# Two directions of an mLSTM folded into one product: the weights scaled by their denominators, the denominators taken two heads at a time, projections placed between the heads

## The chip, the core and the metric

The kernel runs on one core of a Trainium2 chip. The metric is the device time of one execution in microseconds (us); lower is better. The core has an engine for matmuls (TensorE, PE in the rows, its weight loads PEld), three engines for elementwise work (VectorE, DVE; ScalarE, ACT; GpSimd, POOL) and DMA queues that SyncE (SP) issues. Each engine takes its instructions in the order in which the program lists them and waits at each for what it reads and for the buffer that it writes.

## The reference, cut to what matters

The model is a two-layer transformer-like stack over 256 context and 256 latent tokens, 1024 channels wide, batch 1. In each layer one projection feeds three branches (a bidirectional mLSTM, attention in a window, global attention), then come a merge, an output projection and a SwiGLU feed-forward block. The change lies in the mLSTM, with 4 heads of 128 channels. It is written as a scan over blocks:

```python
w = jnp.exp(dlog - m_t[..., None])
s = jnp.einsum('bhtd,bhsd->bhts', qc, kc) * w
num = a[..., None] * jnp.einsum('bhtd,bhde->bhte', qc, C) + jnp.einsum('bhts,bhse->bhte', s, vc)
den = a * jnp.einsum('bhtd,bhd->bht', qc, n) + jnp.sum(s, axis=-1)
hc = num / jnp.maximum(jnp.abs(den), jnp.exp(-m_t))[..., None]
```

It runs once forwards and once backwards in time; the two results are added and then normalised per head, gated by a tanh of another projection (B_O) and projected on. The kernel has no scan: for each head and direction it forms the whole masked matrix of weights, 512 keys by up to 512 queries. In layer 0 the queries are all 512 tokens, in layer 1 only the 256 latent ones.

## The kernel before

**The work around the change.** `layer` (from L964) runs projections with weights split into a high and a low part: `split` makes `whi` by a copy on ACT (L192) and `wlo` by a subtraction on DVE (L193), and each block of the product is three matmuls (two with `whi`, one with `wlo`), all at L135, since a helper issues every matmul. A projection of one 128-channel strip is 24 matmuls. `proj_v` makes the values `v` of all heads, in four PSUM tiles of the pools `mm`, `s`, `mm`, `s`; DVE adds a bias to each and so frees the tile (L417). In layer 0 DVE also computes the modulation vectors of the adaLN by long multiply-and-accumulate passes (L300, tiles `q`, `h`), in blocks that `mod_upto` puts into the stream between the projections; `late` counts them out.

**The mLSTM of a head.** `rep` broadcasts a row of the running maximum over the 128 partitions by a matmul into `tr`; ACT takes exponentials (L590) into eight weight tiles, four blocks of keys (`sb`) by two directions (`d`), direction 0 in `q`, direction 1 in `wk`; POOL cuts the diagonal blocks (L596, L600). PE multiplies keys and queries into `s` (shape `s<-m,m`), and DVE multiplies each score with the weight tile in place (L613). The products with the values go to two PSUM tiles, direction 0 in `acc`, direction 1 in `tr`, and ACT copies each out to `y` (L679).

**Denominators.** For heads 0 to 2 POOL first adds the four weight tiles of a direction (`mlstm_weight_sums`, L637 to L652, into `pv`), and one product with a strip of 32 columns of a constant adds the sum over keys into one of four groups of 32 partitions of a shared PSUM tile `den` (shape 128*32). Head 3 feeds its tiles directly. After the fourth head one chain makes the reciprocals `r` of all heads: copy on ACT, a matmul with C_SUM into `tr`, two DVE operations, the DVE reciprocal (L694). Then `mlstm_sum` per head: two broadcasts of `r`, two DVE multiplies and an add (L703, L704), a square on ACT (L705).

**What sets the order.** The tile framework records the program in the order in which it is written, moved by priority, and puts instructions on each engine in one fixed list. A tile pool with few buffers ties a producer to the last reader of the buffer: PSUM has 3 buffers `mm`, 2 `s`, 2 `tr`, 1 `acc`. In layer 0 the four B_O projections stand ahead of the first score; in layer 1 they come ahead of the gates. The four WQ projections and WK follow heads 2 and 3 and stand between the sums (`other`, L997).

Of the kernel before, what the change touches and what calls it, by code (L numbers as in the profile page):

```python
# [10 lines left out]
F32 = mybir.dt.float32  # L11
# [65 lines left out]
MSB = ((2, 3), (0, 1))  # L77
# [15 lines left out]
class Net:  # L93
    def __init__(self, nc, tc, es, io, out, plan=None):
# [25 lines left out]
        self.low = self.cp.tile([128, 1], F32, name="low")  # L120
        self.ident = self.cst[:, C_ID:C_ID + 128]
# [453 lines left out]

    def mlstm_weights(self, h, n, rows):
# [4 lines left out]
        wt = {}  # L581
        for d in range(2):
            mrep = self.rep(mx, d, h, n)
            for sb in ((2, 3, 0, 1) if d == 0 else (3, 2, 1, 0)):
# [4 lines left out]
                w = self.big("wk" if d else "q")  # L589
                nc.scalar.activation(out=w[:, lo:hi], in_=mrep[:, lo:hi], func=AF.Exp, scale=-1.0,  # L590
                                     bias=ut[:, 64 * sb + 32 * d + h:64 * sb + 32 * d + h + 1])
                if sb < 2 or not lat_only:
# [6 lines left out]
                    else:  # L599
                        self.masked = nc.gpsimd.affine_select(out=w[:, a:a + 128], in_=w[:, a:a + 128],  # L600
                                                              pattern=[[-1, 128]], compare_op=ALU.is_ge, fill=0.0,
                                                              base=0, channel_multiplier=1)
# [3 lines left out]
    def mlstm_scores(self, n, half, q, k, wt):  # L606
        for sb in MSB[half]:
# [8 lines left out]
    def mlstm_values(self, h, n, half, v, wt, num, den):  # L616
        parts = []
        for d in range(2):
            for i, sb in enumerate(MSB[half][::1 - 2 * d]):
                w, lo, hi = wt[d, sb]  # L620
                pieces = [(lo, hi)]
                if d == 0 and sb == 3 and n == T:
                    pieces = [(0, SEQ), (384, 512)]
                for a, b in pieces:
                    self.mm(num[d][:, a:b], v[sb][:, 128 * h:128 * h + 128], w[:, a:b], i + half == 0, i + half == 2)
                    parts.append((d, sb, w, a, b))
        if h < NH - 1:
            return
        for d, sb, w, a, b in parts:
            self.mlstm_den_part(den, h, d, sb % 2, w, a, b, half == 1)  # L630

    def mlstm_den_part(self, den, h, d, i, w, a, b, stop):

        r, c = 4 * d + h, 32 * (2 * i + d)
        self.mm(den[c:c + 32, a:b], self.cst[:, C_STRIP + 31 - r:C_STRIP + 63 - r], w[:, a:b], False, stop)

    def mlstm_weight_sums(self, n, wt):  # L637

        nc = self.nc
        t = self.t("pv", [128, 2 * T])  # L640
        sums = [t[:, :n], t[:, T:T + n]]
        for d in (1, 0):
            out = sums[d]
            order = (2, 3, 0, 1) if d == 0 else (3, 2, 1, 0)
            (w0, _, _), (w1, _, hi) = [wt[d, sb] for sb in order[:2]]
            nc.gpsimd.tensor_tensor(out=out[:, :hi], in0=w0[:, :hi], in1=w1[:, :hi], op=ALU.add)
            if hi < n:
                nc.gpsimd.tensor_copy(out[:, hi:], w0[:, hi:n])
            for sb in order[2:]:
                w, lo, hi = wt[d, sb]  # L650
                nc.gpsimd.tensor_tensor(out=out[:, lo:hi], in0=out[:, lo:hi], in1=w[:, lo:hi], op=ALU.add)
        return sums  # L652

    def mlstm_heads(self, n, q, k, v, rows, den, other):

        nums, prev = [], None
        sums = []
        for h in range(NH + 1):
            for half in range(2):
                if h < NH:  # L660
                    if half == 0:
                        wt = self.mlstm_weights(h, n, rows)
# [644 lines left out]
```

## Time and profile before

| | |
|---|---|
| runs of before | 1457.09 us median (1456.44 to 1457.2, 3 runs) |
| profiled execution | 1458.23 us, its span 1456.5 us |
| TensorE busy, share of the span | 1437.6 us, 99% |
| VectorE busy | 1065.0 us, 73% |
| ScalarE, GpSimd busy | 743.3 us and 55.4 us |
| mLSTM of layer 0 (first score to last value matmul) | about 130 to 171 us of the span |
| mLSTM of layer 1 | about 998 to 1024 us |

The profiled execution is one run with its own time; the span goes from its first to its last instruction. An engine that is busy for 99% of the span leaves hardly anything but its own work to shorten, and any time in which it is kept waiting is added to the end.

### The profile page before, as it was taken

How to read it: one execution, taken by the hardware profiler on the slowest of the kernel's cores; microseconds unless marked ns; L12 is line 12 of the kernel's file. 1: busy time of each engine (PE TensorE's matmuls, PEld its weight loads, DVE VectorE, ACT ScalarE, POOL GpSimd, SP SyncE). 2: the span in 40 equal slices, each digit the busy share in tenths (PEclk: the TensorE clock that was granted, in tenths of full speed). 3: DMA queues.
4: the chain of work that ended last, by engine and by line, in shares of the span. 5: the costliest groups of instructions: out<-in, count | busy, mean ns of one | idle time of the engine just before them, and what ended most of it. 6: DMA issues, size and time to landing. Idle time of an engine off the chain costs nothing.

```text
span 1456.5 us, 24450 instructions
## 1 busy us (share of the span) xinstructions
PE 1437.6 (99%) x8586; PEld 1224.6 (84%) x8586; DVE 1065.0 (73%) x2672; ACT 743.3 (51%) x1525; POOL 55.4 (4%) x111
## 2 busy tenths in 40 slices
PE   8999999999999999999999999999999999999997
PEld 5686687778777889888888888988889889999997
DVE  6595498667698447988688687764899867776775
ACT  4644456557853336332332233755567766655553
POOL 0003300000000000000000000004100000000000
PEclk8999999999999999999999999999999999999998
DMA  9662012222246222666455553241234335555552
GB/s 339 226 210 72 30 47 95 66 73 87 95 145 232 98 84 74 216 203 210 152 188 194 175 173 100 94 152 59 70 103 146 106 111 184 175 183 184 182 176 86
DMA packets 112587, 203.67 MB, mean 140 GB/s; under 512 B 12496, under 2 KB 16336, under 8 KB 112464
## 3 DMA queue, kind: packets, MB, share of 16 engines
q1 hardware_dynamic: 112464, 202.11, 41.7%
q8 instruction: 67, 1.10, 0.3%
q14 instruction: 56, 0.46, 0.1%
HBM read 201.02 MB, written 1.05 MB: 139 GB/s over the span
## 4 chain that ended last, share of the span: by engine, by line
PE 92%; DVE 4%; ACT 2%; issue 1%; DMA 1%; SPq 0%; ACTq 0%; DVEq 0%
PE mm L135 62%; PE s L135 20%; PE acc L135 4%; PE tr L135 4%; PE tr L788 2%; DVE wlo L193 1%; DVE q L488 1%; DMA y<-w_mod 1%; DVE y L703 0%; DVE h L447 0%; ACT q L375 0%; ACT hx L192 0%; ACT q L494 0%; DVE wk L769 0%; DMA wraw<-w_in 0%
## 5 line engine op out<-in xcount | busy, mean ns | idle before, releaser
L192 ACT ACTIVATE whi<-wraw 128x512 fp32r<-128x512 f32 (+1 forms) x558 | 345.0, 624 | 512.7 <-PE mm L135 344.2
L135 PE MATMUL mm<-hx,whi 128*128 128x512 f32 (+2 forms) x2128 | 540.9, 342 | 0.3 <-ACT wk L928 0.2
L193 DVE TENSOR_TENSOR wlo<-wraw,whi 128x512 fp32r<-128x512 f32 (+1 forms) x558 | 374.7, 680 | 163.8 <-ACT whi L192 145.7
L135 PEld LDWEIGHTS mm<-hx,whi 128*128 128x128 f32 x2128 | 365.9, 189 | 50.4 <-issue 5.2
L135 PE MATMUL mm<-hx,wlo 128*128 128x512 f32 (+2 forms) x1064 | 361.3, 340 | 0.0
L135 PE MATMUL mm<-y,whi 128*128 128x256 f32 (+1 forms) x1024 | 260.5, 332 | 0.0
L135 PEld LDWEIGHTS mm<-hx,wlo 128*128 128x128 f32 x1064 | 201.6, 190 | 23.7 <-issue 2.4
L135 PE MATMUL s<-hx,whi 128*128 128x512 f32 (+2 forms) x800 | 192.7, 330 | 0.0
L135 PEld LDWEIGHTS mm<-y,whi 128*128 128x128 f32 x1024 | 176.7, 190 | 17.0
L135 PE MATMUL mm<-y,wlo 128*128 128x256 f32 (+1 forms) x576 | 188.6, 327 | 0.0
L135 PEld LDWEIGHTS s<-hx,whi 128*128 128x128 f32 x800 | 135.9, 190 | 14.1 <-issue 0.4
L135 PE MATMUL s<-hx,wlo 128*128 128x512 f32 (+2 forms) x400 | 132.0, 330 | 0.0
L135 PEld LDWEIGHTS mm<-y,wlo 128*128 128x128 f32 x576 | 109.4, 190 | 9.5
L300 DVE SCALAR_TENSOR_TENSOR q<-q,q 128x512 f32<-128x512 f32 x160 | 105.4, 684 | 0.1
L300 DVE SCALAR_TENSOR_TENSOR h<-q,q 128x512 bf16<-128x512 f32 x160 | 104.7, 684 | 1.0 <-DMA q<-w_mod 1.0
L135 PE MATMUL mm<-m,whi 128*128 128x256 f32 (+1 forms) x320 | 85.2, 320 | 0.0
L135 PEld LDWEIGHTS s<-hx,wlo 128*128 128x128 f32 x400 | 75.7, 189 | 7.1 <-issue 0.4
L135 PE MATMUL s<-q,q 128*128 128x512 f32 (+1 forms) x192 | 66.3, 385 | 0.1
L135 PEld LDWEIGHTS mm<-m,whi 128*128 128x128 f32 x320 | 56.9, 190 | 4.4
L863 DVE SCALAR_TENSOR_TENSOR X<-mm,m,X 128x256 f32<-128x256 f32 x88 | 40.0, 479 | 24.9 <-PE mm L135 24.9
L135 PE MATMUL mm<-whi,hx 128*128 128x256 f32 (+1 forms) x192 | 49.4, 320 | 0.0
L788 PE MATMUL tr<-cst,wk 128*128 128x128 f32 x320 | 49.4, 276 | 0.0
(244 smaller groups left out, 1721.7 us busy)
## 6 DMA issues: line engine op xcount, KB each, us to landing
wraw<-w_ff SPq DMA_DIRECT2D x256, 256.0 KB, 2.9
wraw<-w_in SPq DMA_DIRECT2D x206, 256.0 KB, 2.8
q<-w_mod SPq DMA_DIRECT2D x160, 256.0 KB, 3.0
wraw<-w_br SPq DMA_DIRECT2D x48, 256.0 KB, 2.7
y<-w_mod SPq DMA_DIRECT2D x32, 256.0 KB, 5.4
wraw<-w_o SPq DMA_DIRECT2D x32, 256.0 KB, 2.8
X<-x SPq DMA_DIRECT2D x4, 512.0 KB, 5.6
q<-cc SPq DMA_DIRECT2D x8, 256.0 KB, 5.0
```

The costliest lines, as they stand in the source:

```text
L135: self.nc.tensor.matmul(out, a, b, start=start, stop=stop)
L192: nc.scalar.activation(out=hi, in_=x, func=AF.Copy)
L193: return nc.vector.tensor_tensor(out=lo, in0=x, in1=hi.bitcast(F32), op=ALU.subtract)
L300: nc.vector.scalar_tensor_tensor(out=junk if v == 0 else raw, in0=raw, scalar=1.0, in1=self.cb[v][c], op0=ALU.mult, op1=ALU.mult, accum_ou ...
L488: nc.vector.tensor_tensor(out=x[other], in0=f[own], in1=x[own].bitcast(F32), op=ALU.subtract)
L788: self.nc.tensor.transpose(pt[:, 128 * b:128 * b + 128], p[:, 128 * b:128 * b + 128], self.ident)
L863: nc.vector.scalar_tensor_tensor(out=self.X[:, j, a:b], in0=ps[:, a - c0:b - c0], scalar=self.mod[l][which][:, j, v:v + 1], in1=self.X[:, ...
```

## The change

The order inside the mLSTM is turned round. Before, numerators of both directions are summed over the keys first and divided and added afterwards. Now the denominators come first, from all weight tiles directly (`mlstm_den_sums`: no sums on POOL, 16 strip matmuls per head, two heads per PSUM tile). Then `mlstm_both` multiplies every weight tile with the broadcast reciprocal of its direction (DVE) and adds the narrower direction's tile into the wider one's (POOL), so that `mlstm_values` needs one product with the values per key block, and ACT copies and squares the result out of PSUM. `mlstm_den` runs twice, for heads 0 and 1 and for heads 2 and 3. The weight tiles of direction 1 come from different pools by head (MALT). The B_O projections (in layer 0 all four, in layer 1 two) and the WQ and WK projections become a list `fill` that `mlstm_heads` takes from between its steps. The modulation blocks that stood between the B_O projections of layer 0 all come behind `proj_v`.

```diff
-MSB = ((2, 3), (0, 1))
+MALT = ("wk", "pv", "y", "wk")
...
+    def mlstm_scores(self, h, n, q, k, rows):
+        wt = self.mlstm_weights(h, n, rows)
+        for sb in (2, 3, 0, 1):
...
+    def mlstm_den_sums(self, n, heads, wts):
+
+        den = self.big("mm")
+        self.mm(den[:, :n], self.cst[:, C_STRIP:C_STRIP + 1].to_broadcast([128, 128]), self.cst[:, :n], True, False)
+        for h in heads:
+            for sb in (2, 3, 0, 1):
+                for d in range(2):
+                    w, lo, hi = wts[h][d, sb]
+                    r, c = 4 * d + h, 32 * (2 * (sb % 2) + d)
+                    self.mm(den[c:c + 32, lo:hi], self.cst[:, C_STRIP + 31 - r:C_STRIP + 63 - r], w[:, lo:hi], False,
+                            h == heads[-1] and sb < 2)
+        return den
...
-        nc.vector.tensor_tensor(out=r[:, :n], in0=ps[:64, :n], in1=r[:, :n], op=ALU.max)
+        nc.vector.scalar_tensor_tensor(out=r[:, :n], in0=ps[:64, :n], scalar=self.rest[:64, pair:pair + 1],
+                                       in1=r[:, :n], op0=ALU.max, op1=ALU.max)
...
-    def mlstm_sum(self, h, n, nums, r):
-
-        nc = self.nc
-        a, b = [x[:, :n] for x in nums]
-        for d, x in ((0, a), (1, b)):
-            ps = self.rep(r, d, h, n)
-            nc.vector.tensor_tensor(out=x, in0=x, in1=ps[:, :n], op=ALU.mult)
-        nc.vector.tensor_tensor(out=a, in0=a, in1=b, op=ALU.add)
-        nc.scalar.activation(out=b, in_=a, func=AF.Square)
+    def mlstm_both(self, h, n, wt, r):
+
+        nc = self.nc
+        reps = [self.rep(r, d, h, n) for d in range(2)]
+        for sb in (2, 3, 0, 1):
+            for d in range(2):
+                w, lo, hi = wt[d, sb]
+                nc.vector.tensor_tensor(out=w[:, lo:hi], in0=w[:, lo:hi], in1=reps[d][:, lo:hi], op=ALU.mult)
+            wide = 1 if sb == 1 else 0
+            w, (o, lo, hi) = wt[wide, sb][0], wt[1 - wide, sb]
+            nc.gpsimd.tensor_tensor(out=w[:, lo:hi], in0=w[:, lo:hi], in1=o[:, lo:hi], op=ALU.add)
+        return [wt[1 if sb == 1 else 0, sb][0] for sb in range(4)]
+
+    def mlstm_values(self, h, n, v, ws):
+
+        num = self.big("tr" if h % 2 else "acc")
+        for sb in (2, 3, 0, 1):
+            top = n if sb >= 2 else SEQ
+            self.mm(num[:, :top], v[sb][:, 128 * h:128 * h + 128], ws[sb][:, :top], sb == 2, sb == 1)
+        a, b = [self.big("y") for _ in range(2)]
+        self.nc.scalar.activation(out=a[:, :n], in_=num[:, :n], func=AF.Copy)
+        self.nc.scalar.activation(out=b[:, :n], in_=num[:, :n], func=AF.Square)
+        return a, b
+
+    def mlstm_heads(self, n, q, k, v, rows, fill):
...
+        scores(0)
+        scores(1)
+        den = self.mlstm_den_sums(n, (0, 1), wts)
+        take(1)
+        r = self.mlstm_den(n, 0, den, rows)
+        scores(2)
+        take(2)
+        out(0, r)
+        scores(3)
+        out(1, r)
+        take(1)
+        den = self.mlstm_den_sums(n, (2, 3), wts)
+        r = self.mlstm_den(n, 1, den, rows)
+        take(len(fill) // 2)
+        out(2, r)
+        take(1)
+        out(3, r)
+        take(len(fill))
+        return nums
...
-            to = [self.proj_f(l, B_O + h, hx, n, "y", AF.Tanh) for h in range(NH)]
+            to = [self.proj_f(l, B_O + h, hx, n, "y", AF.Tanh) for h in range(NH // 2)]
...
-        for h in range(NH):
+        for h in range(8):
             late(4 + h)
         if first is not None:
             to = []
-            for h in range(NH):
-                to.append(self.proj_f(l, B_O + h, hx, n, "y", AF.Tanh))
-                late(8 + h)
-
...
+        fill = [lambda h=h: to.append(self.proj_f(l, B_O + h, hx, n, "y", AF.Tanh)) for h in range(len(to), NH)]
+        fill += [lambda h=h: wq.append(self.proj_qk(l, B_WQ + h, hx, n, None)) for h in range(4)]
+        fill.append(lambda: wq.append(self.proj_qk(l, B_WK, hx, T, None, True)))
+        nums = self.mlstm_heads(n, q, k, v, rows, fill)
+        wk = wq.pop()
```

`rest` is a constant of two columns, set up at the start by three small DVE operations; it holds 1 for the heads whose denominators are not in the tile and so keeps the reciprocal finite there.

What stands on TensorE where the mLSTM of layer 0 begins, before: the last of the 96 matmuls of the B_O projections (`mm<-hx`), the transposes of the gates (`tr<-cst,pt`), the constant that opens `den` (`mm<-cst`), two broadcasts (`tr<-pt,sel`) and the first two scores (`s<-m,m`).

```order
L135 MATMUL mm_1279<-hx_269,wlo_1177 128x512
L559 MATMUL tr_1316<-cst,pt_697 128x64 x4
L135 MATMUL mm_1326<-cst 128x512
L135 MATMUL tr_1328<-pt_1323,sel 128x512
L135 MATMUL tr_1342<-pt_1323,sel 128x512
L135 MATMUL s_1356<-m_719,m_727 128x512
L135 MATMUL s_1360<-m_719,m_727 128x512
L135 MATMUL acc_1380<-q_1330,y_1076 128x512
```

The same place after the change. The first row is the last matmul of `proj_v`.

```order
L136 MATMUL s_929<-whi_975,hx_271 128x512
L560 MATMUL tr_1164<-cst,pt_701 128x64 x4
L136 MATMUL s_1202<-m_723,m_731 128x512
L136 MATMUL mm_1260<-cst 128x512
L136 MATMUL s_1206<-m_723,m_731 128x512
L136 MATMUL mm_1290<-hx_256,whi_1005 128x512
L136 MATMUL mm_1290<-hx_257,whi_1005 128x512
```

The transposes and the first score now follow `proj_v` at once, and the B_O projections (`mm_1290` is the first) stand behind the first two scores.

On VectorE, around the four adds of `proj_v` (`y<-mm,n` and `y<-s,n`), before:

```order
L300 SCALAR_TENSOR_TENSOR h_1264,m_143<-q_1262,q_730 128x512
L300 SCALAR_TENSOR_TENSOR q_1257,m_142<-q_1257,q_731 128x512
L417 TENSOR_TENSOR y_1072<-mm_922,n_926 128x512
L417 TENSOR_TENSOR y_1074<-s_923,n_926 128x512
L417 TENSOR_TENSOR y_1076<-mm_924,n_926 128x512
L417 TENSOR_TENSOR y_1078<-s_925,n_926 128x512
L193 TENSOR_TENSOR wlo_1171<-wraw_1169,whi_1170 128x512
```

And after:

```order
L301 SCALAR_TENSOR_TENSOR h_1156,m_143<-q_1154,q_733 128x512
L301 SCALAR_TENSOR_TENSOR q_1149,m_144<-q_1149,q_736 128x512
L418 TENSOR_TENSOR y_1076<-mm_926,n_930 128x512
L418 TENSOR_TENSOR y_1078<-s_927,n_930 128x512
L418 TENSOR_TENSOR y_1080<-mm_928,n_930 128x512
L418 TENSOR_TENSOR y_1082<-s_929,n_930 128x512
L301 SCALAR_TENSOR_TENSOR q_1154,m_143<-q_1154,q_735 128x512
```

The adds kept their place behind the modulation passes; the `wlo` subtractions that followed them before stand further on.

On TensorE, strips of the denominators (32x512 and the like) in layer 0, before, at the end of head 1:

```order
L135 MATMUL tr_1448<-wk_1409,y_1074 128x256
L135 MATMUL tr_1448<-wk_1412,y_1072 128x128
L135 MATMUL mm_1326<-pv_1372,cst 32x512
L135 MATMUL mm_1326<-pv_1439,cst 32x512 x2
L135 MATMUL mm_1581<-hx_256,whi_1219 128x512
```

After, in the middle of heads 0 and 1:

```order
L136 MATMUL s_1210<-m_723,m_731 128x256
L136 MATMUL mm_1260<-wk_1176,cst 32x384
L136 MATMUL mm_1260<-q_1181,cst 32x512
L136 MATMUL mm_1290<-hx_266,wlo_1012 128x512
L136 MATMUL s_1214<-m_723,m_731 128x256
L136 MATMUL mm_1260<-wk_1177,cst 32x512
L136 MATMUL mm_1260<-q_1178,cst 32x256
L136 MATMUL s_1244<-m_725,m_806 128x512
```

The strips of the sums stood together once or twice; the strips of single tiles (`wk`, `q`) now stand one, two or three at a time between full-width matmuls.

## Rows read from the trace of the kernel before

**Rows 1.** The page: span, and busy time of each engine.

```profile
span 1456.5 us, 24450 instructions
...
PE 1437.6 (99%) x8586; PEld 1224.6 (84%) x8586; DVE 1065.0 (73%) x2672; ACT 743.3 (51%) x1525; POOL 55.4 (4%) x111
```

**Rows 2.** Stages: length, busy PE, PEld, DVE, ACT, POOL, clock, DMA share, GB/s.

```profile
60.00:118.00 58.00, 57.48 (x259) 45.56 (x258) 55.18 (x137) 26.12 (x41) 0.00 (x0) 1.00 0.64 218
...
131.00:170.00 39.00, 38.83 (x159) 23.75 (x161) 18.70 (x40) 20.23 (x43) 23.93 (x54) 1.00 0.06 21
170.00:205.00 35.00, 34.43 (x180) 25.87 (x180) 28.31 (x49) 18.21 (x30) 3.65 (x4) 1.00 0.12 39
...
1025.00:1060.00 35.00, 33.58 (x234) 29.64 (x234) 31.52 (x79) 18.71 (x40) 3.21 (x4) 1.00 0.20 65
```

**Rows 3.** Timeline of TensorE: start, us, what (xrecords), idle before and its releaser.

```profile
109.22 0.62 PE L135 MATMUL mm<-hx,whi 128*128 128x512 f32 x2
...
109.90 0.62 PE L135 MATMUL mm<-hx,whi 128*128 128x512 f32 x2
...
145.36 1.88 PE L135 MATMUL s<-m,m 128*128 128x512 f32 x4
147.07 0.59 PE L135 MATMUL acc<-q,y 128*128 128x256 f32 x2
...
176.17 1.07 PE L135 MATMUL tr<-pt,cst 128*64 128x512 f32 x2
```

**Rows 4.** Timeline of TensorE: strips of the denominators and what follows them.

```profile
139.93 1.05 PE L135 MATMUL mm<-pv,cst 128*32 128x512 f32 x2
...
148.80 1.06 PE L135 MATMUL mm<-pv,cst 128*32 128x512 f32 x6
...
166.60 0.62 PE L135 MATMUL mm<-q,cst 128*32 128x512 f32 x2
...
168.44 0.92 PE L135 MATMUL acc<-q,y 128*128 128x256 f32 x4
...
169.94 0.40 PE L135 MATMUL mm<-q,cst 128*32 128x256 f32 x2
...
170.51 0.73 PE L135 MATMUL mm<-hx,whi 128*128 128x512 f32 x2
...
1011.44 0.66 PE L135 MATMUL mm<-pv,cst 128*32 128x256 f32 x8
```

**Rows 5.** Timeline of TensorE: end of `proj_v`, and the gate transposes.

```profile
106.28 0.39 PE L135 MATMUL s<-whi,hx 128*128 128x512 f32 x1
106.50 0.62 PE L135 MATMUL mm<-hx,whi 128*128 128x512 f32 x2
...
128.36 0.46 PE L559 MATMUL tr<-cst,pt 64*128 64x64 f32 x4
```

**Rows 6.** Timeline of VectorE: the first two adds of `proj_v`.

```profile
109.09 0.69 DVE L417 TENSOR_TENSOR y<-mm,n 128x512 f32<-128x512 f32 x1
109.69 0.68 DVE L417 TENSOR_TENSOR y<-s,n 128x512 f32<-128x512 f32 x1
```

**Rows 7.** Groups by shape, 118 to 245 us: busy us, mean ns, idle before.

```profile
L646 POOL TENSOR_TENSOR pv<-wk,wk 128x384 f32<-128x384 f32 x3 | 3.0, 1000 | 0.0
```

**Rows 8.** Timeline of TensorE, layer 1: two waits behind the reciprocals.

```profile
1035.01 0.38 PE L135 MATMUL tr<-pt,sel 128*128 128x256 f32 x1 [0.35 <-DVE y L703]
...
1048.16 0.62 PE L135 MATMUL acc<-y,dup 128*32 128x256 f32 x2 [1.07 <-ACT y L705]
```

**Rows 9.** Timeline of TensorE at the start of the kernel.

```profile
12.78 1.07 PE L135 MATMUL tr<-y,h 128*32 128x256 f32 x16 [0.91 <-DMA y<-w_mod]
```

**Rows 10.** Stages at the start, columns as in rows 2.

```profile
12.00:16.00 4.00, 3.22 (x32) 2.72 (x32) 0.69 (x1) 1.49 (x3) 0.00 (x0) 0.86 1.05 382
...
24.00:26.00 2.00, 2.00 (x6) 1.31 (x6) 1.07 (x5) 1.49 (x4) 0.00 (x0) 0.50 0.66 215
...
28.00:30.00 2.00, 2.00 (x20) 1.06 (x20) 1.02 (x2) 0.54 (x2) 0.00 (x0) 0.86 0.95 306
```

More of the change, by code (lines that the diff above doesn't have):

```diff
@@ L120, in __init__ @@
         self.low = self.cp.tile([128, 1], F32, name="low")
+        self.rest = self.cp.tile([128, 2], F32, name="rest")
         self.ident = self.cst[:, C_ID:C_ID + 128]
@@ L574, in rep, with mlstm_tiles @@
         return ps
+    def mlstm_tiles(self, h):
+        kind = MALT[h]
+        if kind == "pv":
+            pair = [self.t("pv", [128, 2 * T]) for _ in range(2)]
+            alt = [p[:, T * c:T * c + T] for p in pair for c in range(2)]
+        else:
+            alt = [self.big(kind) for _ in range(4)]
+        return [(self.big("q"), alt[sb]) for sb in range(4)]
     def mlstm_weights(self, h, n, rows):
@@ L581, in mlstm_weights @@
         wt = {}
+        tiles = self.mlstm_tiles(h)
         for d in range(2):
@@ L614, in mlstm_scores @@
                                                     in1=w[:, lo:hi], op0=ALU.mult, op1=ALU.mult)
[L616 to L637, printed above, removed]
-        nc = self.nc
[L640 to L662, printed above, removed]
-                    self.mlstm_scores(n, half, q[h], k[h], wt)
-                    if half == 1 and h < NH - 1:
-                        with self.after(self.masked):
-                            sums.append(self.mlstm_weight_sums(n, wt))
-                if prev is not None:
-                    g, ghalf, gwt = prev
-                    if ghalf == 0:
-                        num = [self.big("acc"), self.big("tr")]
-                    if g >= NH - 2 and ghalf == g - (NH - 2):
-                        for i in ((0, 1), (2,))[ghalf]:
-                            for d, w in enumerate(sums[i]):
-                                self.mlstm_den_part(den, i, d, i % 2, w, 0, n, False)
-                    self.mlstm_values(g, n, ghalf, v, gwt, num, den)
-                    if ghalf == 1:
-                        nums.append([self.big("y") for _ in range(2)])
-                        for d in range(2):
-                            self.nc.scalar.activation(out=nums[g][d][:, :n], in_=num[d][:, :n], func=AF.Copy)
-                        other(g)
-                prev = (h, half, wt) if h < NH else None
-        return nums
@@ L684, in mlstm_den @@
-    def mlstm_den(self, n, den, rows):
+        return wt
+    def mlstm_den_sums(self, n, heads, wts):
[9 more added lines that the diff above has]
+        return den
@@ L685, in mlstm_den @@
+    def mlstm_den(self, n, pair, den, rows):
         nc = self.nc
@@ new lines, in mlstm_heads, with take, out @@
+    def mlstm_heads(self, n, q, k, v, rows, fill):
+        wts, nums = {}, []
+        scores = lambda h: wts.update({h: self.mlstm_scores(h, n, q[h], k[h], rows)})
+        def take(m):
+            for f in fill[:m]:
+                f()
+            del fill[:m]
+        def out(h, r):
+            nums.append(self.mlstm_values(h, n, v, self.mlstm_both(h, n, wts.pop(h), r)))
+        scores(0)
[17 more added lines that the diff above has]
+        return nums
@@ L1162, in run @@
                                 negate=True)
+        for i in range(2):
+            nc.vector.tensor_reduce(out=self.rest[:, i:i + 1], in_=ident[:, 0:2, 2 * i:2 * i + 2],
+                                    axis=mybir.AxisListType.XY, op=ALU.add, negate=True)
+        nc.vector.tensor_scalar(out=self.rest, in0=self.rest, scalar1=1.0, scalar2=None, op0=ALU.add)
         nc.vector.memset(self.dup, 0.0)
```

23 lines of the change are left out of this document (4 added, 19 removed).

## The prediction

> **What bounds the kernel now.** I read the page first. TensorE is busy for 1437.6 of 1456.5 us [rows 1]; so a change is worth what it does to the sum of TensorE's own work plus what it does to the waits of TensorE, and nothing else. Next the table by stages around the mLSTM [rows 2]: from 131 to 205 us TensorE is idle for 0.17 + 0.57 = 0.7 us, in the second half of the same stretch of layer 1 (1025 to 1060 us) for 1.4 us. VectorE, ScalarE and GpSimd are each busy for about half or two thirds of the heads' stretch, 18.70, 20.23 and 23.93 us of 39. So work added to them is not paid by itself; it is paid where TensorE stands in line behind it. One stage is different: from 60 to 118 us VectorE is busy for 55.18 of 58 us [rows 2], with the modulation passes, while TensorE is also full. There both engines are at their end, and TensorE is kept fed only because what it does next doesn't need VectorE's latest result. Last I read the timelines for prices.
>
> **Prices.** A matmul of a projection at 512 columns takes 0.227 us: three of them start at 109.22 and the next three at 109.90 [rows 3]. A full-precision matmul (scores, values) leaves two records and takes 0.855 us for 512 columns: two scores start at 145.36 and the next instruction at 147.07 [rows 3]; by columns, 0.43 for 256. The C_SUM product takes 1.07 us at 512 [rows 3], so some 0.5 at 256. A lone strip of a denominator takes 1.05 us at 512 columns, and three of them that follow one another take 1.06 together [rows 4]; four of 256 columns (eight records) take 0.66 [rows 4]. So a group of strips that stand together and fall into different groups of 32 columns costs what one of them costs.
>
> **The change, part by part: TensorE's work.**
> Values: per head 2560 columns in layer 0 become 512 + 512 + 256 + 256 = 1536, in layer 1 1792 become 1024. Four heads save 4096 and 3072 columns, eight and six times 0.855: -6.8 and -5.1 us.
> Opening the second `den` tile: +0.86 and +0.43. Second C_SUM: +1.07 and +0.5.
> Strips: before, layer 0 pays 1.05 and 1.06 for the sums of heads 0 to 2, then 168.44 - 166.60 = 1.84 and 170.51 - 169.94 = 0.57 for the rest of them and head 3 [rows 4], 4.5 us. After, a layer has 32 strips, eight per head, sixteen per `den` tile. In heads 0 and 1 of layer 0, as the listing of the change shows for a part of them, they come in eight separate groups between scores and projection matmuls, six with a strip of 512 columns, one of 256, one of 128. At 1.05, 0.6 and 0.3 that is 7.2 us. Those of heads 2 and 3 stand together; head 3 and one pair of sums took 1.84 + 0.57 = 2.4 us before for eleven strips, so sixteen, in fewer runs, are about 3.2 us. Together 10.4: +5.9 us. Layer 1: before one group of 0.66 and one head's worth of strips, taken as half of layer 0's 2.4 plus the same fixed part, about 2.2; after, fifteen groups, twelve of 256 columns and three of 128 only. At 0.43 and 0.21 (the pitch of a full matmul) they are 5.8 us, at 0.66 and 0.3 they are 8.8; I take 7.2, nearer to the row for a group: +5.0.
> Sum of the work: layer 0 -6.8 + 0.9 + 1.1 + 5.9 = +1.1; layer 1 -5.1 + 0.4 + 0.5 + 5.0 = +0.8. What the product saves, the strips spend. Broadcasts and scores are as many as before, and the projections only move.
>
> **TensorE's waits, layer 0.** `proj_v` ends at about 106.67 (its last matmul starts at 106.28 and is modelled with 0.39) [rows 5], and before the change 96 matmuls of the B_O projections run until the gate transposes at 128.36 [rows 5]. The scores use PSUM tiles `s`, the same two that `proj_v` leaves its results in, and VectorE empties the first of these in the add that starts at 109.69 and takes 0.68 [rows 6], because its modulation passes stand ahead. Before, that was hidden under 22 us of projections. After, the transposes (0.4 us) are followed at once by the first score, which has to wait from 107.1 to 110.4: +3.3 us with nothing behind it that could go ahead, since the queue is in order. In the listing VectorE has as many instructions ahead of the adds as before, so I keep the time. The second score then comes as the last add ends, and the first six matmuls of a B_O projection cover the gate copy and the next VectorE operations. From there the listing gives each exponential and scaling something to hide behind.
> Second wait: the first value product of head 0. After the two broadcasts of the reciprocals it needs two VectorE multiplies (0.6 us each, by the pitch of the adds in rows 6) and a GpSimd add of 384 columns (1.0 us [rows 7]), 2.2 us, and has only two scores (1.7 us) in front: +0.5. Later products have a projection in front. The reciprocals themselves have two projections of 5.4 us as cover; without them the price would be their whole chain. Waits that go: the 0.7 us of rows 2. Net +3.1 us.
>
> **TensorE's waits, layer 1.** No modulation passes stand there. Two waits behind the reciprocal chain, 0.35 and 1.07 us [rows 8], go, because reciprocals come before the values and the square follows a product directly. The lower bound is that nothing replaces them (-1.4), the upper that the same 0.5 us appears at the first product of the first two heads (-0.4). I take -1.2. Two B_O projections that move are the same matmuls in another place.
>
> **VectorE, ScalarE, GpSimd.** Per head VectorE gets eight multiplies in place of two and an add, in layer 0 about 2 us more; GpSimd swaps sums for adds of like size; ScalarE trades squares from SBUF for squares from PSUM. In 131 to 170 us they have 15 to 20 us spare [rows 2]: nothing, unless TensorE stands behind them (rival 3).
>
> **Sum.** 1.1 + 3.1 + 0.8 - 1.2 = +3.8 us on the profiled execution's 1458.23, which is 1.14 above the median of the runs. Against the median: 1457.09 + 3.8 = 1460.9 us, just over 0.2% slower. About 0.2% (2.9 us) is what a measurement of this kernel can tell from no change.
>
> **Rival 1: faster, the strips pack.** A strip needs a quarter of the array's columns. If those that now stand two and three at a time cost a full group only each fourth time, by the 1.06 us for three and 0.66 for four [rows 4], layer 0 would pay about 0.86 + 0.43 per head, 5.2 us, and layer 1 3.4; that is 5.2 and 3.8 below my sum, and the time 1452. Against it: in the listing a full-width matmul stands between most of them. It decides if the sum of the strips' time comes out under some 14 us for both layers. A gain also needs the wait of 3.3 us to be no longer than that.
>
> **Rival 2: slower, the clock.** The wait of 3.3 us is by far the longest idle time of TensorE since the start of the kernel. At the start the granted clock was 0.86 on average from 12 to 16 us, after an idle 0.91 us and then only narrow matmuls [rows 9, 10], then 0.50, that is 1.2 instead of 2.4 GHz, and 0.50 still from 24 to 26 us with TensorE busy for 2.00 of 2.00 us; it rose in the stretch from 28 to 30 us [rows 10]. If it falls again at 110 us, dense matmuls at half speed for some 7 us (as from about 21 to 28 us) cost 3.5 us more: 1464.4. Against it: an idle 3.3 us between dense work is not what stood there. The Trainium skill, "TensorE: Matmul & The Clock Gate", section "Why this matters for your kernels", asks for no idle gaps of TensorE between bursts of matmuls, since the clock drops back after one; this change makes such a gap, and no row here shows one amid dense work.
>
> **Rival 3: slower, the heads starve.** The strips of heads 0 and 1 are in line behind the scaling of their own tile, that behind exponential and mask. If ScalarE's weight copies come between the exponentials, every second of the eight groups waits for about 1 us: +4, 1465. Against: a head's exponentials take less than the 8 us that TensorE spends on a head there, and ScalarE is at 20.23 of 39 us [rows 2].
>
> **How the numbers follow.** Forecast 0.45: of it 0.20 within 0.2%, 0.25 slower, since 1460.9 lies on the edge of 1460.0. Rival 1 0.30: 0.28 faster, 0.02 within. Rival 2 0.15 and rival 3 0.10: slower, but 0.01 of each within. So faster 0.28, within 0.24, slower 0.48. The bounds of the strips (layer 1's 5.8 to 8.8, and layer 0's as much again) and of the waits make the forecast's own range 1457 to 1465. For 8 in 10 the range takes in most of both sides: 1450 to 1467 us.
>
> **What would show it.** Right: TensorE idle for about 3.3 us just after `proj_v` in layer 0, released by the add on VectorE; strips over 15 us in all; value products at 0.855 per 512 columns, 16 a layer; no wait at the squares of layer 1. Wrong: strips that overlap with their neighbours, an idle time that is not there or over 5 us, a granted clock under 1.00 anywhere from 105 to 130 us, or waits between 115 and 132 us of more than 2 us in sum. A cost outside both mLSTM stretches, in the attention of either layer, would be none of these cases.

## The result: slower, and by more than three times what the sum said

| | before | after |
|---|---|---|
| median of the runs | 1457.14 us | 1471.3 us (1469.91 to 1472.06, 4 runs) |
| ratio | | 1.0094, interval 1.0082 to 1.0106 |
| profiled execution and its span | 1458.23, 1456.5 us | 1471.68, 1469.2 us |

The sign was right; +3.8 us became +14, outside the range. The page of after, as in [rows 1]:

```profile
span 1469.2 us, 24490 instructions
...
PE 1446.1 (98%) x8592; PEld 1217.3 (83%) x8592; DVE 1090.3 (74%) x2723; ACT 739.8 (50%) x1521; POOL 56.2 (4%) x104
```

TensorE has 8.5 us more to do and waits 4.2 us more. Where, the table by stages tells (columns as in [rows 2]), cut at the end of `proj_v`, at the first attention score of layer 0, at the gate transposes of layer 1 and at its first attention score. Of before:

```profile
0.00:106.50 106.50, 100.56 (x530) 71.50 (x531) 74.23 (x186) 52.59 (x90) 0.20 (x4) 0.94 0.75 263
106.50:207.80 101.30, 100.56 (x463) 71.81 (x462) 65.36 (x130) 47.93 (x88) 27.68 (x58) 1.00 0.15 50
207.80:997.30 789.50, 788.53 (x4076) 656.83 (x4074) 580.72 (x1543) 366.14 (x743) 3.92 (x5) 1.00 0.41 136
997.30:1052.50 55.20, 53.67 (x345) 45.73 (x345) 40.86 (x101) 32.31 (x76) 19.75 (x39) 1.00 0.16 52
1052.50:1456.00 403.50, 394.24 (x3178) 378.76 (x3176) 303.88 (x718) 244.32 (x528) 3.85 (x5) 0.99 0.45 149
```

The same stages of after:

```profile
0.00:107.00 107.00, 100.98 (x530) 71.24 (x530) 74.68 (x190) 52.58 (x90) 0.20 (x4) 0.94 0.74 259
107.00:218.20 111.20, 104.56 (x461) 67.67 (x461) 85.55 (x163) 46.25 (x86) 28.92 (x53) 0.98 0.16 53
218.20:1001.30 783.10, 782.81 (x4028) 651.08 (x4026) 574.02 (x1527) 363.01 (x737) 4.33 (x5) 1.00 0.41 135
1001.30:1065.40 64.10, 63.68 (x402) 48.29 (x402) 51.69 (x127) 33.53 (x80) 18.89 (x37) 1.00 0.20 67
1065.40:1469.00 403.60, 394.06 (x3178) 378.98 (x3176) 304.33 (x720) 244.44 (x528) 3.84 (x5) 0.99 0.46 148
```

Layer 1's stretch holds two B_O projections that stood ahead of it before, 48 matmuls of 256 columns at 0.12 us (the step of such matmuls among their like), 5.76 us; they are taken out here:

| us | forecast | measured |
|---|---|---|
| layer 0, work of TensorE | +1.1 | +4.0 |
| layer 0, waits | +3.1 | +5.9 (0.74 to 6.64) |
| layer 1, work | +0.8 | +4.2 (63.68 - 5.76 - 53.67) |
| layer 1, waits | -1.2 | -1.1 (1.53 to 0.42) |
| elsewhere | 0 | 0.0 (+0.5 at the start, -0.6 between, +0.1 at the end) |

Two terms hold to 0.1 us; two works and the waits of layer 0 don't. The experiments take these apart.

One caution for their times: the part ahead of the change, up to the last matmul of `proj_v`, took 106.3 us in the profile of before, 106.8 in that of after, and 103.9 to 106.8 in those below, though none of the experiments edits anything there. The granted clock at the start of the kernel differs there, as this stage of after and the same of the shortest (`c_add0`, near the end) show:

```profile
24.00:28.00 4.00, 3.84 (x10) 2.52 (x10) 3.07 (x8) 3.34 (x7) 0.00 (x0) 0.50 0.77 263
```

```profile
24.00:28.00 4.00, 3.55 (x29) 2.10 (x28) 3.68 (x7) 3.16 (x7) 0.00 (x0) 1.00 1.01 360
```

So where a median tells more or less than the edited stretches of the profile do, the stretches are given as well (layer 0: from the last matmul of `proj_v` to the first attention score; layer 1: from the gate transposes to the first attention score).

### The profile page after: what moved, and what is told of

Same layout as the page of the kernel before. It is cut to its first block, busy times and chain, and to the rows that moved or that the text cites. A ratio compares the mean times of both kernels' runs of the same rounds, so it can differ in the third digit from the quotient of the medians.

```text
span 1469.2 us, 24490 instructions
## 1 busy us (share of the span) xinstructions
PE 1446.1 (98%) x8592; PEld 1217.3 (83%) x8592; DVE 1090.3 (74%) x2723; ACT 739.8 (50%) x1521; POOL 56.2 (4%) x104
## 3 DMA queue, kind: packets, MB, share of 16 engines
HBM read 201.02 MB, written 1.05 MB: 138 GB/s over the span
## 4 chain that ended last, share of the span: by engine, by line
PE 91%; DVE 4%; ACT 2%; DMA 1%; issue 1%; SPq 0%; POOL 0%; DVEq 0%; ACTq 0%; POOLq 0%
PE mm L136 62%; PE s L136 19%; PE acc L136 4%; PE tr L136 3%; PE tr L796 2%; DVE wlo L194 1%; DVE q L301 1%; DMA y<-w_mod 1%; DVE h L301 1%; DMA wraw<-w_in 0%; DVE q L489 0%; ACT hx L193 0%; ACT q L376 0%; ACT whi L193 0%; POOL q L668 0%
```

## The idle start and the clock

Timeline of TensorE after the change, just behind the gate transposes (start, us, what, idle before and its releaser):

```profile
110.95 1.82 PE L136 MATMUL s<-m,m 128*128 128x512 f32 x2 [3.41 <-DVE y L418]
112.57 1.91 PE L136 MATMUL mm<-cst 128*128 128x512 f32 x2
114.27 1.22 PE L136 MATMUL s<-m,m 128*128 128x512 f32 x2
```

And stages of 2 us there:

```profile
109.00:111.00 2.00, 0.05 (x1) 0.05 (x1) 1.97 (x5) 0.00 (x0) 0.00 (x0) 1.00 0.00 0
111.00:113.00 2.00, 2.00 (x3) 0.92 (x4) 2.00 (x5) 0.00 (x0) 0.00 (x0) 0.56 0.00 0
113.00:115.00 2.00, 2.00 (x5) 0.77 (x3) 1.95 (x7) 0.00 (x0) 0.00 (x0) 0.59 0.00 0
115.00:117.00 2.00, 2.00 (x10) 1.46 (x9) 1.89 (x3) 0.00 (x0) 0.00 (x0) 1.00 0.08 25
```

The wait of 3.41 us is there, released by the add that the forecast named. In the two stages behind it the granted clock is 0.56 and 0.59, near the lower of its two levels (1.2 GHz), and from 115 us on it is 1.00 again. The score steps (from its start to the next start) 1.62 us and the opening of `den` 1.70 where 0.855 is the price at 2.4 GHz [rows 3], 1.6 us, and 1.8 with what the next instructions lose. Rival 2 is thus no rival but part of the result, at half the price that it had. The Trainium skill, "TensorE: Matmul & The Clock Gate", section "Why this matters for your kernels", asks for no long idle gaps between bursts of matmuls; this gap bears it out.

**One B_O projection ahead of the gates in layer 0.**

```diff
         if first is not None:
-            to = []
+            to = [self.proj_f(l, B_O, hx, n, "y", AF.Tanh)]
         rows = self.gate_finish(*rows)
```

> The changed kernel with one B_O projection of layer 0 put back between the values projection and the first score. Theory of places (each loss has its own place and price): the idle 3.41 us at 107.5 us is covered by 5.4 us of matmuls, the clock stays at 1.00 there (it was 0.56 and 0.59 from 111 to 115 us, worth about 1.8 us), so 5.2 us go: about 1466 us. Rival, VectorE bounds the heads of layer 0 (busy for 85.55 of 111.2 us): TensorE only waits later, at the strips or the value products, and under 2 us go: 1469.5 or more.

Measured: 1467.49 us, 1.0071 (1.0056 to 1.0086). The wait for the add is gone, but TensorE now stands as long for the gate rows, which VectorE gets to later. The timeline, and the stage behind it:

```profile
115.68 0.77 PE L136 MATMUL tr<-pt,sel 128*128 128x512 f32 x1 [2.99 <-DVE pt L569]
```

```profile
115.00:117.00 2.00, 1.32 (x2) 0.83 (x3) 1.97 (x4) 0.00 (x0) 0.00 (x0) 0.59 0.59 205
```

**Fifteen useless matmuls in the idle time.**

```diff
         rows = self.gate_finish(*rows)
+        if first is not None:
+            warm = self.big("acc")
+            for i in range(15):
+                self.mm(warm, hx[0][0][:, :128], hx[i % 8][0], i == 0, i == 14)
```

> The changed kernel with 15 matmuls whose result nobody uses (3.4 us) in layer 0 between the gate transposes and the first score, where TensorE was idle for 3.41 us. They cost nothing if the idle time is VectorE's; the clock should stay at 1.00 from 107 to 117 us. Theory (the clock fell because of the idle time and cost 1.8 us): 1469.5. Rival (the fall has another cause, the clock falls all the same): 1471.3. The order of the strips after it changes too and may move 1 to 3 us, so the granted clock is what decides.

Measured: 1472.75 us, 1.0102 (1.0087 to 1.0118): nothing won. The first wait shrinks to 0.15 us, and 3.02 us appear one step on, for the same gate rows; the clock falls there, to 0.80 from 113 to 115 us and 0.50 from 115 to 117, while it stays at 1.00 from 107 to 113, where the idle time was filled. So VectorE, not the order on TensorE alone, sets this place: whatever stands ahead, the gate rows come when the modulation passes let them.

**Gate transposes first, then one B_O projection, then the scores.**

```diff
         rows = self.gate_finish(*rows)
+        for h in range(1 if first is not None else 0):
+            to.append(self.proj_f(l, B_O + h, hx, n, "y", AF.Tanh))
```

> The changed kernel with only the start of layer 0's mLSTM edited: gate transposes, one B_O projection, then the first score. In the run with the projection ahead of the transposes the wait only moved (2.99 us) and the clock fell all the same. Theory (the price is the idle time plus the clock that falls after it): here the wait is 1.9 us as in combo1 and the clock stays at 1.00, so 1.5 us of idle time and 1.8 us of clock go, and with fewer single strips some 1 to 2 us more: 1467 us. Rival (the clock falls in any case): 1469.5.

Measured: 1465.66 us, 1.0053 (1.004 to 1.0066), 5.6 us less than after. One wait of 1.86 us is left, for the gate rows, and the stages that hold it and what follows are at full clock:

```profile
113.00:115.00 2.00, 0.36 (x2) 0.35 (x3) 1.95 (x5) 0.51 (x1) 0.00 (x0) 1.00 0.00 0
115.00:117.00 2.00, 2.00 (x7) 1.00 (x6) 2.00 (x4) 1.85 (x5) 1.09 (x2) 1.00 0.33 84
```

In these four kernels the clock fell behind waits of 3.41, 2.99 and 3.02 us and not behind one of 1.86. The length of a wait alone doesn't decide, though. In `strips_few`, the run of the next section that leaves strips out, the clock fell a second time, in the attention of layer 1, behind a wait of 1.59 us and about 1 us of matmuls of two columns:

```profile
1068.39 1.05 PE L136 MATMUL tr<-cst,n 128*128 128x2 f32 x8 [1.59 <-ACT n L466]
```

```profile
1068.00:1072.00 4.00, 3.61 (x21) 3.61 (x22) 2.49 (x12) 2.79 (x8) 0.00 (x0) 0.67 0.37 131
```

## The strips

A head has eight strips, not the 16 that the section on the change gives it, and a pair of heads sixteen.

**Strips of a pair issued after its last score**, so that they stand together.

```diff
...
-            self.mm(s[:, :top], k[...], q[:, :top], True, True)
+            self.last = self.mm(s[:, :top], k[...], q[:, :top], True, True)
...
+                    with self.after(self.last):
                         self.mm(den[c:c + 32, lo:hi], ...)
```

> The changed kernel with the strips of the denominators of each pair of heads issued behind the last score of the pair, so that they stand together. Theory of places: a group of four strips costs what its longest strip costs; heads 0 and 1 of layer 0 paid 6.8 us in eight groups and should pay 3.4, layer 1 paid 8.4 us in fifteen groups and should pay 4.0; no new wait: about 8 us go, 1463. Rival: with the strips in one heap TensorE has to wait at the heap for VectorE's last scalings, 1 to 2 us for each of the four heaps, and the reciprocals come later: 1 to 3 us go, 1469.

**Twelve of the sixteen strips of a pair left out.**

```diff
-        for h in heads:
-            for sb in (2, 3, 0, 1):
+        for h in heads[-1:]:
+            for sb in (0, 1):
```

> The changed kernel without 12 of the 16 strips of each pair of heads; those of the last two key blocks of the second head stay, so that the reciprocals are still made behind the last scaling. It leaves out most of the sum in the denominators. Theory of places: the strips are TensorE's own work, 10.5 us in layer 0 and 8.4 us in layer 1; about 1 us of each stays; 17 us go: 1454. Rival, VectorE: the strips filled time in which TensorE would wait for scalings anyway; 8 us go or less, 1463 or more, and TensorE shows waits of several us at the scores and value products.

Measured: grouped 1459.55 us, 1.0011 (1.0001 to 1.0021); few 1456.14 us, 0.9989 (0.998 to 0.9998). Between after and grouped lie 11.8 us: 5.3 in layer 0's stretch, 5.5 in layer 1's, the rest ahead of the change. So the mere place of the strips is worth 10.8 us, most of the loss. From the first score to the first attention score of layer 0, and the same stretch as above of layer 1, of after, grouped and few in turn (the second figure is TensorE's busy time):

```profile
110.90:218.20 107.30, 104.02 (x456) 67.35 (x457) 81.68 (x151) 45.62 (x85) 28.92 (x53) 0.98 0.17 55
1001.32:1065.40 64.08, 63.66 (x402) 48.29 (x402) 51.67 (x127) 33.53 (x80) 18.89 (x37) 1.00 0.20 67
```

```profile
109.90:211.86 101.96, 98.70 (x457) 67.76 (x457) 81.38 (x151) 45.42 (x85) 28.94 (x53) 0.98 0.19 58
994.76:1053.38 58.62, 57.18 (x401) 47.61 (x401) 52.67 (x128) 33.40 (x80) 18.54 (x37) 1.00 0.22 68
```

```profile
109.02:206.45 97.43, 93.95 (x409) 65.29 (x409) 81.30 (x151) 45.51 (x85) 28.96 (x53) 0.98 0.19 61
989.93:1047.20 57.27, 56.20 (x354) 46.84 (x353) 50.80 (x124) 33.83 (x80) 18.98 (x37) 1.00 0.22 69
```

Grouping takes 5.3 us of work from layer 0 and 6.5 from layer 1, with as many strips; in layer 1 waits of 1.0 us come up in their place. Leaving out 24 of a layer's 32 takes 10.1 and 7.5, and the two stretches become 16.7 us shorter together, for the 17 that was expected; no new wait of TensorE comes up in layer 0. The profiled execution as a whole is 13.7 us shorter: the part ahead of the change is 1.9 us shorter too, but the part behind layer 1's first attention score, which holds the wait of 1.59 us and the low clock shown above, is 4.4 longer. I had set all 32 at 10.4 and 7.2, so the price of the other eight, in a few groups, is missing there. Timeline of grouped, sixteen strips of heads 0 and 1 of layer 0 in 2.71 us, the first record and what comes behind the last:

```profile
126.01 0.62 PE L136 MATMUL mm<-q,cst 128*32 128x512 f32 x1
...
128.72 1.13 PE L136 MATMUL s<-m,m 128*128 128x512 f32 x2
```

In after the eight groups of these sixteen take 6.8 us by their steps. And the steps are not all. Two places of after, one in each layer, each with one lone strip:

```profile
119.52 1.05 PE L136 MATMUL mm<-q,cst 128*32 128x512 f32 x2
120.50 0.50 PE L136 MATMUL mm<-hx,wlo 128*128 128x512 f32 x1
120.84 0.62 PE L136 MATMUL mm<-hx,whi 128*128 128x512 f32 x2
...
1038.95 0.27 PE L136 MATMUL mm<-hx,whi 128*128 128x256 f32 x1
1039.16 0.62 PE L136 MATMUL mm<-q,cst 128*32 128x256 f32 x2
1039.71 0.38 PE L136 MATMUL mm<-hx,whi 128*128 128x256 f32 x1
1039.93 0.28 PE L136 MATMUL mm<-hx,wlo 128*128 128x256 f32 x1
```

The strip of 512 columns steps 0.98 us, but the projection matmul behind it 0.34 where 0.227 is its like's step. The strip of 256 columns steps 0.55, but the matmul ahead of it 0.21 and the one behind it 0.22 where 0.12 is their like's step: from 1038.95 to 1039.93 us the three take 0.98, and without the two at 0.12 the strip costs 0.74 us. For a group of 256 columns I had 0.43 to 0.66. Priced in this way, every piece between two rows of projection matmuls that holds strips, less its other matmuls at their own steps, the strips cost about 12.7 us in layer 0 and 11.3 in layer 1 of after, against 6.0 and 3.6 of before. This is an estimate; it gives +6.7 and +7.7 us where the forecast had +5.9 and +5.0.

## The waits at heads 2 and 3 of layer 0

Timeline of after, the waits in layer 0 behind the start:

```profile
151.85 1.13 PE L136 MATMUL acc<-q,y 128*128 128x512 f32 x2 [0.44 <-POOL q L668]
187.01 1.13 PE L136 MATMUL acc<-q,y 128*128 128x512 f32 x2 [1.31 <-POOL q L668]
189.22 1.13 PE L136 MATMUL acc<-q,y 128*128 128x512 f32 x2 [0.16 <-POOL q L668]
200.91 1.53 PE L136 MATMUL tr<-q,y 128*128 128x512 f32 x3 [1.31 <-DVE wk L665]
```

The first is the one of the forecast, 0.44 for 0.5. The other three, 2.8 us, were not in it. GpSimd's adds (L668) and VectorE's scalings (L665) release them. VectorE, between the scalings of head 2 (L665), does the rotary work of the WQ projections that have become its neighbours (L446 to L489). Timeline of VectorE, and of GpSimd:

```profile
182.42 1.40 DVE L489 TENSOR_TENSOR q<-n,q 64x512 fp32r<-64x512 f32 x2 [0.76 <-ACT q L488]
...
187.33 2.38 DVE L489 TENSOR_TENSOR q<-n,q 64x512 fp32r<-64x512 f32 x2
```

```profile
187.38 1.79 POOL L668 TENSOR_TENSOR q<-q,y 128x512 f32<-128x512 f32 x1 [0.42 <-DVE y L665]
```

The same two multiplies take 1.40 us alone and 2.38 with a GpSimd add running. Not every VectorE operation is stretched: a scaling of 128x512, which reads one operand from PSUM, took 0.68 us at 186.03, inside a GpSimd add of 128x384, as without one.

**Scalings of heads 2 and 3 written ahead of a projection.**

```diff
         take(len(fill) // 2)
-        out(2, r)
+        ws = self.mlstm_both(2, n, wts.pop(2), r)
         take(1)
-        out(3, r)
+        nums.append(self.mlstm_values(2, n, v, ws))
+        ws = self.mlstm_both(3, n, wts.pop(3), r)
+        take(1)
+        nums.append(self.mlstm_values(3, n, v, ws))
```

> The changed kernel with the scaling of the weights of heads 2 and 3 written ahead of a projection, the value products behind it, so that 5 us of matmuls of a projection stand between the broadcasts of the reciprocals and the product. Theory of places: the waits of 1.31, 0.16 and 1.31 us at the value products of heads 2 and 3 of layer 0 go, 2.8 us: 1468.5. Rival, VectorE: its rotary work of the projections and the scalings fill it from 172 to 205 us, the wait moves to the squares or the attention scores: no change, 1471.

Measured: 1469.64 us, 1.0082 (1.0067 to 1.0097), 1.7 us less than after at intervals that overlap. In the profile the gain is smaller still: layer 0's stretch is 1.1 us shorter, layer 1's 0.6 longer, and 1.7 us lie ahead of the change, where nothing was edited. Waits in layer 0 behind the start fall from 3.2 to 2.4 us (1.4 for GpSimd, 1.0 for VectorE), and 0.5 comes up in layer 1. Of the 2.8 us that were expected to go 0.8 did, and the rival is nearer: written order alone doesn't clear VectorE.

## A reading that fell: the projections in pieces

Summed from start to start, the 288 projection matmuls of layer 0's stretch had become 3.9 us longer than in before, those of layer 1's 2.8: each reduced-precision matmul behind a full-precision one steps 0.42 us instead of 0.227. I took that for a price of turning from one kind to the other, and tried it alone, in layer 1 ahead of the gates.

```diff
         if first is None:
...
+            fast = lambda i: self.mm(pa, hx[i % 8][0][:, :128], hx[i % 8][1], i == 0, i == 15)
+            slow = lambda i: self.mm(pb, self.cst[:, :128], self.cst[:, 128:640], i == 0, i == 15)
...
```

Sixteen of each, pinned in their order: first all fast, then all slow; and in turns.

> The changed kernel, with 32 useless matmuls added ahead of the second layer's gate arithmetic, whose operands lie ready: first sixteen of the kind that the projections use (reduced precision, 512 columns), then sixteen of full precision (512 columns), in that order. Border theory: sixteen at the step that such matmuls have among their like (0.227 us) and sixteen at 0.855 us, about 17.3 us more than the changed kernel, with one border between the two kinds. Rival (the extra time of the projections' pieces is waiting for operands): the same 17.3 us; this kernel is the measure for the other one.

> The same 32 useless matmuls at the same place, taking turns: one of reduced precision, one of full precision, sixteen times. Border theory: each reduced-precision matmul behind a full-precision one takes 0.42 us in place of 0.227, and each full-precision one behind a reduced-precision one some 0.04 us more, so this kernel is 3 to 4 us longer than the one with two blocks (ratio between them 1.002 to 1.003). Rival (waiting for operands): no operand is waited for here, so the two kernels agree within 0.5 us.

Measured: 1489.31 us, 1.0227 (1.0204 to 1.025), and 1489.03 us, 1.0214 (1.0199 to 1.0229): no difference. Timeline of the blocks, and what follows them:

```profile
1001.02 3.79 PE L136 MATMUL acc<-hx,hx 128*128 128x512 f32 x16
1004.65 13.89 PE L136 MATMUL tr<-cst 128*128 128x512 f32 x32
1018.47 0.46 PE L560 MATMUL tr<-cst,pt 64*128 64x64 f32 x4
```

Of the turns, the first two:

```profile
1000.24 0.39 PE L136 MATMUL acc<-hx,hx 128*128 128x512 f32 x1
1000.47 1.02 PE L136 MATMUL tr<-cst 128*128 128x512 f32 x2
1000.92 0.80 PE L136 MATMUL acc<-hx,hx 128*128 128x512 f32 x1
1001.56 1.02 PE L136 MATMUL tr<-cst 128*128 128x512 f32 x2
```

A fast (reduced-precision) one and a slow (full-precision) one step 0.227 + 0.864 = 1.09 us in blocks; in turns the fast one steps 0.64 and the slow one 0.455, 1.09 again; 17.45 and 17.58 us in all. The record of a matmul behind a slow one begins while that one still runs, so a step from start to start moves 0.4 us from the slow one to the fast one. The border costs nothing that could be measured; the projections do only move, as the forecast said, and what seemed theirs belongs to the products and strips in between.

## Put together

**One projection between transposes and scores, strips grouped, scalings early** (the edits above), with one projection and with two:

> The changed kernel with three edits together: strips grouped behind the last score of each pair, scalings of heads 2 and 3 ahead of a projection, and in layer 0 the gate transposes first, then one B_O projection, then the first score. Theory of places: the gains add, 11.8 (strips) + 1.7 (scaling) + 5.2 (idle 3.4 and clock 1.8; the wait of 2.99 us for the split row maxima of the run with one projection ahead does not come, since the transposes no longer stand behind the projection): 1452.6 us, faster than before. Rival, VectorE bounds the heads: the gains overlap, 1457 or more, with a wait of some us at the broadcasts of the row maxima or the heap of strips.

> As combo1 with two B_O projections of layer 0 ahead of the first score. If one projection (5.4 us) covers VectorE's adds and the split of the row maxima, this gives the same within 1 us or loses up to 1.5 us, since one projection less stands between the heads: 1452.6 to 1454. If VectorE is still behind after 5.4 us, it is up to 2 us faster than combo1.

Measured: 1456.81 us, 0.9994 (0.9986 to 1.0003), and 1459.41 us, 1.0013 (1.0004 to 1.0021). With one projection the 14 us lost are back, but the repairs don't add up in full: 18.7 us were expected, 14.5 came, and the rival (1457 or more) is nearer. What they take from TensorE's own work stays (6.9 us in layer 0, 6.4 in layer 1); of the waits 4.7 us are left in layer 0, 1.3 of them new, at the products of the squares, for ScalarE (L680), and 1.5 in layer 1. A second projection ahead makes TensorE stand for the exponentials (1.7 us, L602), and layer 0's stretch 2.1 us longer; a wait of 1.3 us for GpSimd in layer 1 stands with one projection too (1.4).

**The adds of `mlstm_both` on VectorE**, in both layers on top of the second, in layer 0 alone on top of the first (the diff is the second of these; the first has `nc.vector` for both layers):

```diff
-            nc.gpsimd.tensor_tensor(out=w[:, lo:hi], in0=w[:, lo:hi], in1=o[:, lo:hi], op=ALU.add)
+            eng = nc.vector if n == T else nc.gpsimd
+            eng.tensor_tensor(out=w[:, lo:hi], in0=w[:, lo:hi], in1=o[:, lo:hi], op=ALU.add)
```

> As combo2 with the adds of the two directions on VectorE in place of GpSimd. If the hop to GpSimd (1.1 to 1.8 us an add) and its hold on VectorE (two multiplies took 2.38 us beside it and 1.40 without) make the waits at the value products, these go: 1 to 3 us faster than combo2. Rival, VectorE's own load decides: 6 us more in layer 0 and 4 in layer 1 on VectorE make it 1 to 3 us slower.

> As combo1 with the adds of the two directions on VectorE in layer 0 alone. combo2_dve, with all adds there, took 100.5 us from the gate transposes to the first attention score of layer 0, where combo1 took 102.3, and lost 3.1 us behind the first attention score of layer 1. If the gain belongs to layer 0 and the loss to layer 1: 2 us faster than combo1, 1455. If VectorE's load in layer 0 decides: 1457 or more.

Measured: 1457.39 us, 1.0001 (0.9992 to 1.001), and 1451.36 us, 0.9963 (0.9951 to 0.9975). With the adds of both layers on VectorE layer 0's stretch is 4.2 us shorter than without and layer 1's 0.7, but the part behind layer 1's first attention score 3.7 longer, for a cause that stays open. The second kernel has the lowest median of all, 0.4% below before. Of the 5.5 us between it and the first of the two put together, layer 0's stretch gives 3.0, for the 2 that were expected; 2.6 lie ahead of the change in the profile. Its three pairs of rotary multiplies, two of them where after had 2.38 and 2.28 us:

```profile
174.45 1.40 DVE L489 TENSOR_TENSOR q<-n,q 64x512 fp32r<-64x512 f32 x2 [0.76 <-ACT q L488]
...
179.22 1.39 DVE L489 TENSOR_TENSOR q<-n,q 64x512 fp32r<-64x512 f32 x2
...
186.42 1.39 DVE L489 TENSOR_TENSOR q<-n,q 64x512 fp32r<-64x512 f32 x2 [0.21 <-ACT q L488]
```

VectorE does more and is done sooner. Two waits are left in layer 0, 1.9 us for the gate rows and 1.0 for VectorE's add, and 1.4 for GpSimd in layer 1.

**Two attempts on these waits**: the gate rows at a higher priority, and with it the later projections moved one place back, so that the last of them stands behind the value products of head 3 (the second diff, its lines against the first attempt).

```diff
-        return ut, self.stack_rows(mx, T), bc
+        with self.urgent(URGENT):
+            rows = self.stack_rows(mx, T)
+        return ut, rows, bc
```

```diff
-        take(1)
+        take(n == SEQ)
         den = self.mlstm_den_sums(n, (2, 3), wts)
         r = self.mlstm_den(n, 1, den, rows)
-        take(len(fill) // 2)
+        take(1 + (n == T))
...
-        take(1)
+        take(n == T)
         nums.append(self.mlstm_values(3, n, v, ws))
```

> As c_add0 with the split of the row maxima (one copy on ScalarE, one subtraction on VectorE) put ahead of the modulation passes on VectorE. If the wait of 1.87 us at the first broadcast comes from VectorE's line of modulation passes and from nothing else, it goes: 1453. If the scores then wait for the values' adds or the exponentials, under 0.7 us go: 1454.5.

> As c_urgent with the WQ projections of layer 0 moved by one place, so that one stands behind the value products of head 3, where the squares waited for ScalarE for 1.3 us. If that wait only lacked cover: 1452. If the cover is now missing at the reciprocals of heads 2 and 3: as c_urgent or up to 1 us slower, 1453 to 1454.

Measured: 1454.03 us, 0.9976 (0.9967 to 0.9984), and 1451.92 us, 0.996 (0.9949 to 0.9972). The start wait stays at 1.7 and 1.9 us, now for the copy of the transposed gates (L562 there), which stands ahead of the gate rows on VectorE: urgency moved the name, not the time. In the profile the first attempt agrees with the kernel without it within 0.1 us in both layers' stretches; its 2.7 us more lie in the main ahead of the change (106.6 us against 103.9). The last is level with the best, with a layer 0 that is 1.5 us shorter than the first attempt's, though not for the expected reason: the wait of 1.3 us at the squares was that of the kernel with GpSimd's adds and had gone with them. What went is a wait of 1.2 us for VectorE's add, with 0.6 new at a broadcast of the reciprocals, and 1.1 us of work, since the small products of the squares (128*32) now stand together: sixteen records in 1.22 us, where the first attempt had them in three groups of 1.05, 0.62 and 0.62.

## Why the forecast fell short, point by point

- **The idle start**: right, 3.41 us for 3.3, with the releaser named.
- **The clock**: the step that set it aside as a rival with 0.15, because no row showed an idle time amid dense work, failed. It came, at 1.8 us instead of 3.5, and went with the idle time when one projection stood in it (1.00 behind a wait of 1.86 us).
- **"Later products have a projection in front"**: failed, 2.8 us in layer 0. A projection in front covers TensorE's wait only if VectorE gets no work from it; the WQ projections bring rotary work, and GpSimd's adds beside it stretch that. With the scalings early and the adds on VectorE 1.0 of the 2.8 us is left. In layer 1 the term held (-1.1 for -1.2).
- **Strips**: the mis-sized term. Layer 1: 24 strips alone are 7.5 us where 7.2 stood for 32, and by the estimate all 32 are 11.3, over the bound of 8.8 too. Layer 0: 10.1 us for 24 where 10.4 stood for 32, by the estimate 12.7. Before was underpriced too (4.5 and 2.2, by the estimate 6.0 and 3.6), so 0.8 us of layer 0's excess and 2.7 of layer 1's are theirs. The step that failed was the price of a group: 0.43 to 0.66 us for 256 columns, read from the group's own row, where the matmuls ahead of it and behind it lose 0.1 us each as well; a lone one costs 0.74. The four strips of 0.66 us in [rows 4] were such a row.
- **Layer 0's work**, +2.9 over the sum: the clock's 1.8, and about 1 for the strips.
- **Values, openings, "the projections only move"**: nothing found against them; without the strips and the clock, TensorE's work comes to the forecast within 0.7 us by the estimate.
- **Rival 1**: strips that stand together do pack, 2.71 us for sixteen; but the change doesn't put them together. The sum of their time was far over its deciding point of 14 us.

Excess: 2.8 (waits) + 1.8 (clock) + 0.8 and 2.7 (strips, by the estimate) = 8.1 of the 9.2 us between sum and table (13.0 - 3.8). The other 1.1 us were not taken apart.

## What to carry to other kernels

Small matmuls on few columns of the array were cheap in company here and dear alone: place them together before counting what a restructured product saves. Where a step moves into another's cover, list what that cover itself gives VectorE and GpSimd to do. And price an interruption from the last of a row of equal matmuls before it to the second one after it, not from record to record.

## What the runs showed of the hardware

- A GpSimd add of 128x512 stretches a pair of VectorE multiplies of 64x512 from 1.40 to 2.38 us, and an add of 128x384 does not stretch a scaling of 128x512 that reads PSUM (0.68 us); on VectorE itself such an add takes 0.68.
- The granted clock of a stage of 2 us went to 0.50 to 0.59 behind an idle 3 us amid dense work and was back at 1.00 some 4 us later (1.8 us lost). Behind an idle 1.86 us it stayed at 1.00; behind an idle 1.59 us and about 1 us of matmuls of two columns it fell (0.67 over 4 us).
- A lone strip of 32 array columns and 256 columns of data cost TensorE 0.74 us between projection matmuls; sixteen strips of 128 to 512 columns together took 2.71 us.
- Turning between reduced and full precision costs TensorE nothing that could be measured: 0.13 us between one turn and thirty-one.
